# A three-product matmul order, the seams' sums, and the last loop step of a causal convolution

## The chip, the cores and the metric

One core of a Trainium2 chip runs the whole program. The metric is the device time of one execution in microseconds; the time before is the median of three executions. The engines that matter are PE (TensorE, the matmuls), DVE (VectorE), ACT (ScalarE) and SP, which issues the DMAs.

## The reference

Two layers, each a feed-forward part, a token mixer and another feed-forward part, on x of 512 tokens by 1024 channels in float32. Layer 0 mixes with a diagonal state-space model (S5), layer 1 with a causal depthwise convolution of 31 taps. Cut to what is computed:

```python
def swiglu(h, w1, w3, w2):
    return (silu(h @ w1) * (h @ w3)) @ w2

def s5_mixer(h, ...):
    u = h @ w_in
    ...
    z = y * sigmoid(y @ w_glu + b_glu)
    return z @ w_out

def conv_mixer(h, ...):
    a, g = split(h @ w_in + b_in, 2)
    z = a * sigmoid(g)
    z = causal_depthwise_conv(z, dw) + dw_b
    z = silu(layernorm(z, ln_g, ln_b))
    return z @ w_out + b_out

for i in range(2):
    h = swiglu(rmsnorm(x, norm_pre[i, 0]), ffn_w1[i, 0], ffn_w3[i, 0], ffn_w2[i, 0])
    x = x + 0.5 * rmsnorm(h, norm_post[i, 0])
    h = s5_mixer(rmsnorm(x, ...)) if i == 0 else conv_mixer(rmsnorm(x, ...))
    x = x + rmsnorm(h, norm_post[i, 1])
    h = swiglu(rmsnorm(x, norm_pre[i, 2]), ffn_w1[i, 1], ffn_w3[i, 1], ffn_w2[i, 1])
    x = x + 0.5 * rmsnorm(h, norm_post[i, 2])
```

## The kernel before

Channels lie on the 128 partitions, tokens in the free dimension; x is eight tiles of 128x512. Every large product is made from three fp32r matmuls (`mm3`, L115): the weight tile and the data are each split into a high part and a rest, and hi·xh, hi·xl and lo·xh are summed in one PSUM bank. L117, L118 and L119 are these three, in that order; L118 is the only one that reads xl, L119 the only one that reads lo. 

Weights come in units of 128x1024 float32 (512 KB), eight 128x128 tiles each, numbered through the program. `want(n)` (L97) splits all units up to n: ACT copies the high part (L101, CAST), DVE subtracts to get the rest (L105). The raw unit comes by a DMA that SP issues (L90). There are three raw buffers, so unit u+3 can be fetched only when the DVE subtraction of unit u has ended, and SP, which issues in program order, waits for it there. Each engine runs its instructions in the order in which the code emits them; that order, and nothing else, is what the change edits.

A sub-layer ends in `proj` (L262), whose last one or two outputs (`nl` of them) are made in two halves of 256 tokens, A and B, so that the norm of half A can start while half B is still being multiplied. Between two sub-layers lies a seam: a loop over `s`, two halves by eight k, in which `scaled` (L358) and `added` (L362) bring x up to date, `split_hi` (ACT, L180) and `split_lo` (DVE, L193) split it, and `entry_step` (L197) multiplies the piece with the first four weight units of the next sub-layer, twelve matmuls at a time. `stat` (L124) sums squares over the partitions with a matmul of ones; `rsqrt_steps` turns them into the factor y. With `defer`, the squares and sums of the new x are made behind the seam (128x512 each) instead of in it, and `entry_norm` (L245) makes y later, in the next sub-layer's loop. The six sub-layers are ffn, S5, ffn, ffn, conv, ffn, so there are five seams; seams 2 (after S5) and 5 (after conv) have nl=2, the others 1.

In S5, `glu_step` multiplies the gate's weights with one k of y for four outputs; `gates` then runs Sigmoid (ACT L1089), a product (DVE L1090), and a split of z (ACT L1093, DVE L1094). The output projection starts with a lead: for each k, four outputs of three matmuls, with the units of s_w_out that `want` splits behind the first gates.

In conv, the loop over i (2 to 7) multiplies 2 x 8 x 3 matmuls for output pair i on PE. On the other engines the pair before is gated (`gate`, DVE L1148 to L1164) and convolved. Channels 0, 1 and (26 taps of it) 7 are convolved on DVE, one tap an instruction (L1183, 128x512); the rest go over DRAM (`z_d`) into a layout in which PE convolves them with Toeplitz operators (`operators` fetches them, 2.25 MB for a channel tile; `banded` L1286 multiplies; `unstack` and `fetch` bring the result back over `c_d`). At i=7 the order is: operators(5), operators(6), `want(u0+19)`, which splits the first four units of the output projection (16 to 19), then `fetch`, gate(6), the taps that are due, and unstack of channel tile 4. After the loop come gate(7) and what is left of the taps and sums, and then a layer norm in two halves (L1403 to L1440), behind which the output projection starts.

Of the kernel before, what the change touches and what calls it, by code (L numbers as in the profile page):

```python
# [13 lines left out]
NK = 8  # L14
# [27 lines left out]
def trunk(ctx: ExitStack, tc: tile.TileContext, h, plan):  # L42
# [72 lines left out]
    def mm3(out, u, s, xh, xl, start, stop):  # L115
        hi, lo = halves[u]
        PE.matmul(out, lhsT=hi[:, s, :], rhs=xh, start=start, stop=False)  # L117
        PE.matmul(out, lhsT=hi[:, s, :], rhs=xl, start=False, stop=False)  # L118
        PE.matmul(out, lhsT=lo[:, s, :], rhs=xh, start=False, stop=stop)  # L119


    def stat(acc):
# [72 lines left out]
        )  # L195

    def entry_step(k, cs, xn, u0, ps4, outs=range(4)):  # L197
        for j in outs:
            mm3(ps4[j][:, cs], u0 + j, k, xn[k][:, 0, cs], xn[k][:, 1, cs], k == 0, k == NK - 1)

    def start(pre):

# [47 lines left out]

        rsqrt(stat(e["acc2"][:, HALVES[1]]), e["y"][:, HALVES[1]])

    def proj(u0, nk, rhs, post, nl, pre, xn, bias=None, lead=None, carried=None, defer=True, early=False):

        acc = stat_tile() if carried is None else carried
        acc2 = stat_tile()
# [2 lines left out]
        un = u0 + nk  # L259
# [28 lines left out]
        if lead is not None:  # L288
            want(unit(3, nk - 1)[0])
            ps4 = [psum() for _ in range(4)]  # L290
            for s in range(2 * nk + 2):
                ck = lead(s)
                if ck:
                    for m in range(4):
                        product(m, ck[1], ps4[m][:, ck[0]], ck[0])
            want(unit(4, nk - 1)[0])
            for m in range(4):
                evac(m, ps4[m], FULL)
                copy(m, ps4[m], FULL)
# [24 lines left out]
        for m in last:  # L324
# [2 lines left out]
                product(m, k, ps, A)  # L327
            evac(m, ps, A)
            copy(m, ps, A)
        psb = {}  # L330
        for i, (m, k) in enumerate((m, k) for m in last for k in range(nk)):
            if i == 5:
                sa = stat(acc[:, A])
                steps = rsqrt_steps(sa, y[:, A], carried is None)
                if pre is not None:
                    lo_engine[0] = None
                    want(un + 3)
                    lo_engine[0] = DVE
                for f in steps:
                    f()  # L340
            if k == 0:
                psb[m] = psum()[:, :n]
            product(m, k, psb[m], B)
            if k == nk - 1 and m != NK - 1:
                evac(m, psb[m], B)
                copy(m, psb[m], B)
        pb = psb[NK - 1]
        if pre is None:
            assert bias is None and carried is not None
# [21 lines left out]
        for s in range(len(todo) + 2):  # L371
            if s < len(todo):
                if s == NK:
                    while side:
                        side.pop(0)()
                scaled(*todo[s])
            if side:
                side.pop(0)()
            elif more and s > NK + 5:
                more.pop(0)()  # L380
            if 1 <= s <= len(todo):
                added(*todo[s - 1])
            if s == 4:
                sq = square(NK - 1, pb, B)
                plus(sq, B)
                sb = stat(acc[:, B])
            if s == 5:
                copy(NK - 1, pb, B)
            if s >= 2:
                cs, k = todo[s - 2]  # L390
                split_lo(k, cs, xn, pre)
                if s == 2:
                    want_late()
                if not defer:
                    x_plus(sqs.pop((cs.start, k)), cs, acc2)
                entry_step(k, cs, xn, un, ps4)
                if early and s == NK + 2:
                    ye = y_tile()
                    more = rsqrt_steps(stat(acc2[:, A]), ye[:, A])
            if s == 5:  # L400
                side = rsqrt_steps(sb, y[:, B], carried is None)
        if defer:
            want(un + 4)
            for k in range(NK):
                x_plus(x_square(k, FULL, acc2), FULL, acc2)
        return {"xn": xn, "ps": ps4, "acc2": acc2, "u": un, "y": ye}
# [477 lines left out]
    def s5(e, post, pre):  # L884
# [125 lines left out]

        def glu_step(j0, bank, k):
            if k >= 0:
                for j in range(4):
                    glu_part(j0, bank, j, k)

        def glu_part(j0, bank, j, k):
            mm3(bank[j], g0 + j0 + j, k, yhl[k][:, 0, :], yhl[k][:, 1, :], k == 0, k == NK - 1)
# [110 lines left out]
    def conv(e, post, pre):  # L1128
# [197 lines left out]
        for i in range(2, NK):  # L1326
            want(u0 + 2 * i + 1)
            pa, pb = psum(), psum()
            for j, ps in enumerate((pa, pb)):
                for k in range(NK):  # L1330
                    mm3(ps, u0 + 2 * i + j, k, xn[k][:, 0, :], xn[k][:, 1, :], k == 0, k == NK - 1)
                    if i == 2 and j == 0 and k == 4:
                        entry_norm(e)
                if j == 0 and i - 3 in banks:
                    done = banded(i - 3)
            if i - 2 in banks and i > 4:
                operators(i - 2)
            if i == NK - 1:
                operators(i - 1)
            want(u0 + 2 * i + (3 if i < NK - 1 else 5))  # L1340
            if i == 2:
                ACT.preload_act_table(AF.Sigmoid)
                for n in range(2):
                    gate(n, e["ps"][2 * n], e["ps"][2 * n + 1])
            else:
                fetch()
                gate(*pend)
            pend = i, pa, pb
            finish()
            if i == NK - 1:  # L1350
                dg = flat(page(F32))
                nc.sync.dma_start(out=dg[:, : (CONV_W - C_TAPS[i]) * P], in_=h["diag"])
            step(BUD_D[i - 2])
            accumulate()
            if done:
                unstack(*done)
                done = None
        done = [banded(i) for i in banks[-2:]]
        fetch()
        gate(*pend)  # L1360
# [45 lines left out]
        first = newton(0)  # L1406
        for n, c in enumerate(HALVES):
            ACT.activation(q[:, c], ps12[n][:, :256], AF.Square, scale=1.0 / 32)
            if n:
                first.pop(0)()  # L1410
            DVE.tensor_tensor(v[:, c], ps12[n][:, 256:], q[:, c], op=S)
            ACT.activation(y0[:, c], v[:, c], AF.Abs_reciprocal_sqrt, bias=eps)
            if n == 0:
                less(0, 0)
        ACT.preload_act_table(AF.Silu)
        for f in first:
            f()
# [61 lines left out]
    for i, (kind, idx) in enumerate(subs):  # L1479
        pre = subs[i + 1][1] * 8 if i + 1 < len(subs) else None  # L1480
        post = 48 + idx * 8
        if kind == "ffn":
            after = subs[i + 1][0] if i + 1 < len(subs) else "ffn"
            e = ffn(e, post, pre, after == "ffn", after == "s5")
        elif kind == "s5":
            e = s5(e, post, pre)
        else:
            e = conv(e, post, pre)
# [101 lines left out]
```

## Time and profile before

| | us |
|---|---|
| median of three executions | 1881.44 (1881.33 to 1881.71) |
| the profiled execution | 1881.37 |
| its span, first to last instruction | 1879.6 |
| DVE busy in the span | 1079.2 |
| ACT busy in the span | 639.1 |

The profiled execution's time is 1.8 us more than its span; that part lies around the instructions. Starts in the timeline are counted from the span's start. PE's ends are modelled and overlap: a row of PE tells by its start, not by its length, and the distance of two starts is the rate. A row of another engine with xN is N instructions that followed each other. The view by windows gives, for a stretch of time, the busy time and number of instructions of each engine, then the granted TensorE clock, the DMA share and GB/s.

### The profile page before, as it was taken

How to read it: one execution, taken by the hardware profiler on the slowest of the kernel's cores; microseconds unless marked ns; L12 is line 12 of the kernel's file. 1: busy time of each engine (PE TensorE's matmuls, PEld its weight loads, DVE VectorE, ACT ScalarE, POOL GpSimd, SP SyncE). 2: the span in 40 equal slices, each digit the busy share in tenths (PEclk: the TensorE clock that was granted, in tenths of full speed). 3: DMA queues.
4: the chain of work that ended last, by engine and by line, in shares of the span. 5: the costliest groups of instructions: out<-in, count | busy, mean ns of one | idle time of the engine just before them, and what ended most of it. 6: DMA issues, size and time to landing. Idle time of an engine off the chain costs nothing.

```text
span 1879.6 us, 24042 instructions
## 1 busy us (share of the span) xinstructions
PE 1861.2 (99%) x9498; PEld 1588.4 (85%) x9498; DVE 1079.2 (57%) x1907; ACT 639.1 (34%) x931; POOL 30.5 (2%) x56
## 2 busy tenths in 40 slices
PE   9999999999999999999999999999999999999998
PEld 7888888888989888888898888888887988888887
DVE  6888556789658543332485433325988775433324
ACT  5232545242245432221344222213413543222211
POOL 0000000003100000000000000000000000000000
PEclk9999999999999999999999999999999999999999
DMA  5344448849422423222223332222473224332321
GB/s 164 113 138 155 146 124 256 279 148 353 152 90 79 135 90 110 92 78 90 102 78 124 102 100 82 95 92 79 163 282 107 79 74 129 97 105 79 95 96 46
DMA packets 101809, 234.87 MB, mean 125 GB/s; under 512 B 26176, under 2 KB 45120, under 8 KB 101696
## 3 DMA queue, kind: packets, MB, share of 16 engines
q1 hardware_dynamic: 101552, 233.31, 38.0%
q8 instruction: 74, 1.21, 0.3%
q14 instruction: 39, 0.32, 0.1%
q10 hardware_dynamic: 144, 0.02, 0.0%
HBM read 209.58 MB, written 23.72 MB: 124 GB/s over the span
## 4 chain that ended last, share of the span: by engine, by line
PE 83%; DVE 12%; ACT 2%; issue 2%; DMA 1%; SPq 0%; DVEq 0%; ACTq 0%
PE ps L118 26%; PE ps L119 26%; PE ps L117 26%; DVE pg L105 1%; DVE pg L697 1%; PE ps L1286 1%; PE ps L976 1%; DVE pg L1183 1%; PE ps L792 1%; DVE pg L527 1%; DVE tmp L467 1%; PE ps L124 1%; ACT tmp L466 1%; DVE pg L699 1%; ACT pg L469 1%
## 5 line engine op out<-in xcount | busy, mean ns | idle before, releaser
L117 PE MATMUL ps<-pg,pg 128*128 128x512 f32 (+1 forms) x2808 | 1035.6, 369 | 4.5 <-ACT pg L1429 3.9
L118 PE MATMUL ps<-pg,pg 128*128 128x512 f32 (+1 forms) x2808 | 1030.8, 367 | 4.5 <-DVE pg L193 3.7
L119 PE MATMUL ps<-pg,pg 128*128 128x512 f32 (+1 forms) x2808 | 1028.5, 366 | 0.2 <-DVE pg L105 0.2
L118 PEld LDWEIGHTS ps<-pg,pg 128*128 128x128 f32 x2808 | 530.7, 189 | 94.7 <-DVE pg L193 7.5
L117 PEld LDWEIGHTS ps<-pg,pg 128*128 128x128 f32 x2808 | 530.8, 189 | 91.5 <-ACT pg L1429 4.3
L119 PEld LDWEIGHTS ps<-pg,pg 128*128 128x128 f32 x2808 | 530.6, 189 | 85.8 <-DVE pg L105 0.9
L105 DVE TENSOR_TENSOR pg<-raw,pg 128x1024 fp32r<-128x1024 f32 x305 | 361.2, 1222 | 106.2 <-ACT pg L101 68.0
L101 ACT CAST pg<-raw 128x1024 fp32r<-128x1024 f32 x310 | 311.4, 1047 | 107.3 <-PE ps L118 28.4
L467 DVE TENSOR_TENSOR tmp<-ps,tmp 128x512 f32<-128x512 f32 x88 | 60.9, 692 | 247.6 <-PE ps L119 218.4
L278 DVE TENSOR_TENSOR acc<-acc,tmp 128x512 f32<-128x512 f32 (+1 forms) x53 | 32.6, 615 | 250.1 <-ACT tmp L273 250.0
L466 ACT ACTIVATE tmp<-tmp 128x512 f32<-128x512 f32 x88 | 55.6, 632 | 287.0 <-DVE tmp L465 287.0
L469 ACT CAST pg<-tmp 128x512 fp32r<-128x512 f32 x88 | 54.6, 621 | 251.2 <-DVE tmp L467 249.4
L273 ACT ACTIVATE tmp<-ps 128x512 f32<-128x512 f32 (+1 forms) x45 | 24.2, 539 | 285.3 <-PE ps L119 284.9
L470 DVE TENSOR_TENSOR pg<-tmp,pg 128x512 fp32r<-128x512 f32 x88 | 61.0, 693 | 61.7 <-ACT pg L469 61.7
L465 DVE TENSOR_TENSOR tmp<-ps,y 128x512 f32<-128x512 f32 x88 | 60.6, 689 | 27.4 <-PE ps L119 27.4
L180 ACT ACTIVATE pg<-x,gsc 128x256 fp32r<-128x256 f32 x80 | 40.7, 509 | 68.1 <-DVE x L362 68.1
L1183 DVE SCALAR_TENSOR_TENSOR pg<-pg,vec,pg 128x512 f32<-128x512 f32 x82 | 55.4, 755 | 0.0
L193 DVE SCALAR_TENSOR_TENSOR pg<-x,gsc,pg 128x256 fp32r<-128x256 f32 (+1 forms) x88 | 44.8, 509 | 2.6 <-ACT pg L180 1.4
L1286 PEld LDWEIGHTS ps<-pg,pg 128*128 128x128 f32 x360 | 40.8, 192 | 0.3
L1286 PE MATMUL ps<-pg,pg 128*128 128x128 f32 x360 | 40.8, 275 | 0.0
L362 DVE SCALAR_TENSOR_TENSOR x<-tmp,gsc,x 128x256 f32<-128x256 f32 x80 | 38.8, 485 | 0.0
L976 PE MATMUL ps<-pg,pg 128*128 128x128 f32 x256 | 35.0, 277 | 1.2 <-DVE pg L962 0.9
(165 smaller groups left out, 828.6 us busy)
## 6 DMA issues: line engine op xcount, KB each, us to landing
raw<-w SPq DMA_DIRECT2D x262, 512.0 KB, 4.0
pg<-tab_d SPq DMA_DIRECT2D x24, 512.0 KB, 5.9
pg<-toep SPq DMA_DIRECT2D x20, 512.0 KB, 6.1
tab_d<-pg SPq DMA_DIRECT2D x16, 512.0 KB, 4.4
raw<-cv_w_in SPq DMA_DIRECT2D x16, 512.0 KB, 4.2
pg<-s5b SPq DMA_DIRECT2D x8, 512.0 KB, 6.5
pg<-f_d SPq DMA_DIRECT2D x32, 128.0 KB, 5.9
raw<-s_w_in SPq DMA_DIRECT2D x8, 512.0 KB, 3.8
```

Of the source, the lines that this page charges most:

```text
L101: ACT.copy(hv, r)
L105: lo_engine[0].tensor_tensor(lv, r, hv.bitcast(F32), op=ALU.subtract)
L117: PE.matmul(out, lhsT=hi[:, s, :], rhs=xh, start=start, stop=False)
L118: PE.matmul(out, lhsT=hi[:, s, :], rhs=xl, start=False, stop=False)
L119: PE.matmul(out, lhsT=lo[:, s, :], rhs=xh, start=False, stop=stop)
L465: DVE.tensor_tensor(a, pa, e["y"], op=ALU.mult)
L466: ACT.activation(a, a, AF.Silu)
L467: DVE.tensor_tensor(a, pb, a, op=ALU.mult)
L469: ACT.copy(t[:, 0, :], a)
L470: DVE.tensor_tensor(t[:, 1, :], a, t[:, 0, :].bitcast(F32), op=ALU.subtract)
L1183: DVE.scalar_tensor_tensor(a, v, dw(i, w), a, op0=M, op1=A)
L1286: PE.matmul(ps[:, q * P : q * P + P], lhsT=op[ND * q + d], rhs=z[:, q, 8 - d : 8 - d + P], start=d == 0, stop=d == ND - 1,)
```

## The change

`mm3` makes hi·xh, lo·xh, hi·xl instead of hi·xh, hi·xl, lo·xh. A new `mm3s` does the same for several outputs at once: first hi·xh and lo·xh of all of them, then hi·xl of all. `entry_step`, the lead of `proj` and S5's `glu_step` use it, with four outputs (the program's start with two and one).

At seams with nl=2, the statistic of half A is made two products earlier (i=3 for i=5); of output 6's half B only the square (ACT) stays where it was, and its sum and its copy (DVE) move into the seam's step s=2.

Into conv, `defer` is 5: the squares and sums of x move out of seam 4 behind the split of the sixth unit, and `entry_norm` moves from the fifth product of i=2's first output to the seventh of its second one, ten products later. The seams after the other feed-forward layers keep what they had (0 before S5, 4 between two).

In conv's step i=7, operators(6) and the four splits move to the end of the step, behind gate(6), the taps and unstack. In the layer norm behind the loop, both squares and variances are made before the two Abs_reciprocal_sqrt, and the first Newton step no longer stands between them.

```diff
@@ mm3 @@
         PE.matmul(out, lhsT=hi[:, s, :], rhs=xh, start=start, stop=False)
-        PE.matmul(out, lhsT=hi[:, s, :], rhs=xl, start=False, stop=False)
-        PE.matmul(out, lhsT=lo[:, s, :], rhs=xh, start=False, stop=stop)
+        PE.matmul(out, lhsT=lo[:, s, :], rhs=xh, start=False, stop=False)
+        PE.matmul(out, lhsT=hi[:, s, :], rhs=xl, start=False, stop=stop)
+
+    def mm3s(todo, xh, xl, start, stop):
+
+        for out, u, s in todo:
+            hi, lo = halves[u]
+            PE.matmul(out, lhsT=hi[:, s, :], rhs=xh, start=start, stop=False)
+            PE.matmul(out, lhsT=lo[:, s, :], rhs=xh, start=False, stop=False)
+        for out, u, s in todo:
+            PE.matmul(out, lhsT=halves[u][0][:, s, :], rhs=xl, start=False, stop=stop)
@@ entry_step @@
-        for j in outs:
-            mm3(ps4[j][:, cs], u0 + j, k, xn[k][:, 0, cs], xn[k][:, 1, cs], k == 0, k == NK - 1)
+        mm3s([(ps4[j][:, cs], u0 + j, k) for j in outs], xn[k][:, 0, cs], xn[k][:, 1, cs], k == 0, k == NK - 1)
@@ proj @@
-                    for m in range(4):
-                        product(m, ck[1], ps4[m][:, ck[0]], ck[0])
+                    c, k = ck
+                    outs = [(ps4[m][:, c], *unit(m, k)) for m in range(4)]
+                    mm3s(outs, rhs[k][:, 0, c], rhs[k][:, 1, c], k == 0, k == nk - 1)
...
-        psb = {}
+        psb, behind = {}, []
...
-            if i == 5:
+            if i == (5 if nl == 1 else 3):
...
             if k == nk - 1 and m != NK - 1:
-                evac(m, psb[m], B)
-                copy(m, psb[m], B)
+                behind.append((m, square(m, psb[m], B)))
...
+            if s == 2 and behind:
+                m, sq = behind.pop()
+                plus(sq, B)
+                copy(m, psb[m], B)
             if s == 4:
...
         if defer:
-            want(un + 4)
+            want(un + defer)
@@ s5 @@
         def glu_step(j0, bank, k):
             if k >= 0:
-                for j in range(4):
-                    glu_part(j0, bank, j, k)
+                mm3s([(bank[j], g0 + j0 + j, k) for j in range(4)], yhl[k][:, 0, :], yhl[k][:, 1, :], k == 0, k == NK - 1)
@@ conv @@
-                    if i == 2 and j == 0 and k == 4:
+                    if i == 2 and j == 1 and k == 6:
                         entry_norm(e)
...
-            if i == NK - 1:
-                operators(i - 1)
-            want(u0 + 2 * i + (3 if i < NK - 1 else 5))
+            if i < NK - 1:
+                want(u0 + 2 * i + 3)
...
                 unstack(*done)
                 done = None
+            if i == NK - 1:
+                operators(i - 1)
+                want(u0 + 2 * i + 5)
...
-            if n:
-                first.pop(0)()
             DVE.tensor_tensor(v[:, c], ps12[n][:, 256:], q[:, c], op=S)
-            ACT.activation(y0[:, c], v[:, c], AF.Abs_reciprocal_sqrt, bias=eps)
             if n == 0:
                 less(0, 0)
+        for c in HALVES:
+            ACT.activation(y0[:, c], v[:, c], AF.Abs_reciprocal_sqrt, bias=eps)
@@ main @@
-            e = ffn(e, post, pre, after == "ffn", after == "s5")
+            e = ffn(e, post, pre, {"ffn": 4, "conv": 5, "s5": 0}[after], after == "s5")
```

Three places show how instructions move. The lines of the changed kernel have other numbers: its matmuls L125 and L126 are hi·xh and lo·xh of `mm3s`, L128 its hi·xl; L133 is the statistic that was L124, L1159 and L1161 the gate's L1148 and L1150, L1257 the sum that was L1246.

First DVE, at conv's step i=7, from the four splits (L105, units 16 to 19) on. Before:

```order
L105 TENSOR_TENSOR pg_11177<-raw_10878,pg_11176 128x1024
L105 TENSOR_TENSOR pg_11183<-raw_11017,pg_11182 128x1024
L105 TENSOR_TENSOR pg_11189<-raw_11023,pg_11188 128x1024
L105 TENSOR_TENSOR pg_11195<-raw_11180,pg_11194 128x1024
L1148 TENSOR_TENSOR tmp_11206<-ps_10917,y_10541 128x512
L1150 TENSOR_TENSOR tmp_11205<-ps_10916,y_10541 128x512
L1153 SCALAR_TENSOR_TENSOR tmp_11205<-tmp_11205,vec,tmp_11206 128x512
L1156 MEMSET pg_11212 128x4x8
L1227 TENSOR_TENSOR pg_10482<-pg_10482,acc_10486 128x512
L1225 SCALAR_TENSOR_TENSOR pg_10483<-pg_10483,vec,acc_10486 128x512
L1245 TENSOR_TENSOR pg_10487<-pg_10482,pg_10483 128x512
L1246 TENSOR_TENSOR pg_10487<-pg_10487,tmp_11222 128x512
```

The next row there is gate(7)'s first, L1148. With the change, from gate(6)'s second row on:

```order
L1161 TENSOR_TENSOR tmp_11149<-ps_10894,y_10549 128x512
L1164 SCALAR_TENSOR_TENSOR tmp_11149<-tmp_11149,vec,tmp_11150 128x512
L1167 MEMSET pg_11156 128x4x8
L1238 TENSOR_TENSOR pg_10472<-pg_10472,acc_10476 128x512
L1236 SCALAR_TENSOR_TENSOR pg_10473<-pg_10473,vec,acc_10476 128x512
L1256 TENSOR_TENSOR pg_10477<-pg_10472,pg_10473 128x512
L1257 TENSOR_TENSOR pg_10477<-pg_10477,tmp_11166 128x512
L105 TENSOR_TENSOR pg_11185<-raw_10856,pg_11184 128x1024
L105 TENSOR_TENSOR pg_11191<-raw_10995,pg_11190 128x1024
L105 TENSOR_TENSOR pg_11197<-raw_11001,pg_11196 128x1024
L105 TENSOR_TENSOR pg_11203<-raw_11188,pg_11202 128x1024
L1159 TENSOR_TENSOR tmp_11288<-ps_11048,y_10549 128x512
```

The four splits stood ahead of gate(6) and now stand behind it and its sums, directly ahead of gate(7) (the last row).

Second PE, at the first step of S5's output lead: banks ps_4764 to ps_4767 are the four outputs, pg_4645 is z's first tile, and pg_4702/4703, pg_4708/4709, pg_4714/4715, pg_4720/4721 are the hi and lo of four weight units. Before:

```order
L117 MATMUL ps_4764<-pg_4645,pg_4702 128x512
L118 MATMUL ps_4764<-pg_4645,pg_4702 128x512
L119 MATMUL ps_4764<-pg_4645,pg_4703 128x512
L117 MATMUL ps_4765<-pg_4645,pg_4708 128x512
L118 MATMUL ps_4765<-pg_4645,pg_4708 128x512
L119 MATMUL ps_4765<-pg_4645,pg_4709 128x512
L117 MATMUL ps_4766<-pg_4645,pg_4714 128x512
L118 MATMUL ps_4766<-pg_4645,pg_4714 128x512
L119 MATMUL ps_4766<-pg_4645,pg_4715 128x512
L117 MATMUL ps_4767<-pg_4645,pg_4720 128x512
L118 MATMUL ps_4767<-pg_4645,pg_4720 128x512
L119 MATMUL ps_4767<-pg_4645,pg_4721 128x512
```

With the change:

```order
L125 MATMUL ps_4764<-pg_4645,pg_4702 128x512
L126 MATMUL ps_4764<-pg_4645,pg_4703 128x512
L125 MATMUL ps_4765<-pg_4645,pg_4708 128x512
L126 MATMUL ps_4765<-pg_4645,pg_4709 128x512
L125 MATMUL ps_4766<-pg_4645,pg_4714 128x512
L126 MATMUL ps_4766<-pg_4645,pg_4715 128x512
L125 MATMUL ps_4767<-pg_4645,pg_4720 128x512
L126 MATMUL ps_4767<-pg_4645,pg_4721 128x512
L128 MATMUL ps_4764<-pg_4645,pg_4702 128x512
L128 MATMUL ps_4765<-pg_4645,pg_4708 128x512
L128 MATMUL ps_4766<-pg_4645,pg_4714 128x512
L128 MATMUL ps_4767<-pg_4645,pg_4720 128x512
```

The fourth unit's lo (pg_4721) was read by the twelfth matmul of the step and is now read by the eighth; the four products with z's low part stand at the end.

Third PE, in conv's step i=2: the statistic from which y is made (acc_9362), between the products of the two outputs. Before, in the first output:

```order
L117 MATMUL ps_10522<-pg_8248,pg_10488 128x512
L118 MATMUL ps_10522<-pg_8248,pg_10488 128x512
L119 MATMUL ps_10522<-pg_8248,pg_10489 128x512
L124 MATMUL ps_10539<-acc_9362,ones 128x512
L117 MATMUL ps_10522<-pg_8317,pg_10488 128x512
L118 MATMUL ps_10522<-pg_8317,pg_10488 128x512
L119 MATMUL ps_10522<-pg_8317,pg_10489 128x512
```

With the change, in the second output:

```order
L117 MATMUL ps_10501<-pg_8386,pg_10444 128x512
L118 MATMUL ps_10501<-pg_8386,pg_10445 128x512
L119 MATMUL ps_10501<-pg_8386,pg_10444 128x512
L133 MATMUL ps_10547<-acc_9362,ones 128x512
L117 MATMUL ps_10501<-pg_8455,pg_10444 128x512
L118 MATMUL ps_10501<-pg_8455,pg_10445 128x512
L119 MATMUL ps_10501<-pg_8455,pg_10444 128x512
```

The statistic stands 30 matmuls of 128x512 later in PE's order.

More of the change, by code (lines that the diff above doesn't have):

```diff
@@ L251, in entry_rest, with proj @@
         rsqrt(stat(e["acc2"][:, HALVES[1]]), e["y"][:, HALVES[1]])
-    def proj(u0, nk, rhs, post, nl, pre, xn, bias=None, lead=None, carried=None, defer=True, early=False):
+    def proj(u0, nk, rhs, post, nl, pre, xn, bias=None, lead=None, carried=None, defer=4, early=False):
         acc = stat_tile() if carried is None else carried
@@ L457, in last_half, with ffn @@
             added(B, k)
-    def ffn(e, post, pre, defer=True, early=False):
+    def ffn(e, post, pre, defer=4, early=False):
         u0, xn = e["u"], e["xn"]
```

## The prediction

> **What bounds the kernel now.** I read the page's busy times and the chain that ended last, then PE's waits, then the stretches where PE is not dense.
>
> ```profile
> PE 1861.2 (99%) x9498; PEld 1588.4 (85%) x9498; DVE 1079.2 (57%) x1907; ACT 639.1 (34%) x931; POOL 30.5 (2%) x56
> PE 83%; DVE 12%; ACT 2%; issue 2%; DMA 1%; SPq 0%; DVEq 0%; ACTq 0%
> ...
> PE ps L117 <- ACT pg L1429: 3.9, 1, 3.9
> PE ps L118 <- DVE pg L193: 3.7, 11, 0.6
> ```
>
> PE is busy nearly all the time, but the second line says that 12% of the chain runs through DVE: there PE keeps busy without setting the end. The waits name few places: the layer norm's first row (L1429), and xl (L193) eleven times, at the seams. No matmul is removed, so the change can only gain what is lost at such places, or lose at places that are dense.
>
> **The rate.** Two starts tell it.
>
> ```profile
> 530.04 0.39 PE L117 MATMUL ps<-pg,pg 128*128 128x512 f32 x1
> 530.27 0.39 PE L118 MATMUL ps<-pg,pg 128*128 128x512 f32 x1
> ...
> 531.63 0.39 PE L118 MATMUL ps<-pg,pg 128*128 128x512 f32 x1
> ...
> 532.86 0.50 PE L119 MATMUL ps<-pg,pg 128*128 128x512 f32 x1 [0.16 <-DVE pg L105]
> 533.20 0.40 PE L117 MATMUL ps<-pg,pg 128*128 128x512 f32 x1
> ```
>
> A 128x512 matmul takes (531.63-530.04)/7 = 0.227 us, whether its weights repeat those before (L117 to L118) or not (L118 to L119); a new order by itself costs nothing. A 128x256 takes 0.12 (574.83 to 574.95 in the next fence).
>
> **Seams.** Windows give what each lost: the stretch less its matmuls at 0.12.
>
> ```profile
> 386.00:410.00 24.00, 23.03 (x174) 21.42 (x173) 21.71 (x59) 12.24 (x30) 0.11 (x1) 1.00 0.37 141
> 570.00:582.00 12.00, 10.53 (x79) 9.62 (x78) 9.53 (x24) 4.53 (x10) 0.00 (x0) 1.00 0.31 102
> 1300.00:1316.00 16.00, 15.37 (x118) 14.35 (x118) 14.78 (x39) 7.42 (x20) 0.00 (x0) 1.00 0.10 33
> 1500.00:1510.00 10.00, 8.32 (x61) 7.46 (x60) 9.03 (x23) 3.74 (x9) 0.00 (x0) 1.00 0.17 60
> ...
> 574.83 0.28 PE L118 MATMUL ps<-pg,pg 128*128 128x256 f32 x1
> 574.95 0.28 PE L119 MATMUL ps<-pg,pg 128*128 128x256 f32 x1
> ...
> 578.35 0.39 PE L118 MATMUL ps<-pg,pg 128*128 128x256 f32 x1 [0.57 <-DVE pg L193]
> ...
> 580.35 0.70 PE L124 MATMUL ps<-acc,ones 128*128 128x256 f32 x2 [0.42 <-DVE acc L278]
> ```
>
> Seam 1 lost 24.0-174x0.12 = 3.1, seam 2 2.5, seam 4 1.8, seam 5 2.7; some tenths of each are the float32 statistics.
> - Seam 1 (into S5): the first product with xl was second in its step and is ninth, 7x0.12 = 0.84 later. DVE keeps its work, and the lateness on it adds up along the seam, so I take **-0.8**; 0 to -2.4 (most of its loss) are the ends.
> - Seams 2 and 5: the statistic of A is two products earlier, and the sum and copy (two rows of some 0.33 us) are out of the way of the first `scaled`. But they come back at s=2 ahead of split_lo, and the first step now needs the fourth unit's lo at its eighth matmul. What is late next is the statistic of B (580.35), behind ACT's square. **-0.6** and **-0.55**, ends 0 and -1.5 each.
> - Seam 3: waits show nothing there; 0.
> - Seam 4: without squares PE leaves it up to 1.9 earlier; but conv behind it is bound by DVE (below), so 0 of its own.
> - The program's start: its pieces need lo0 a matmul earlier and xl later; **-0.1**.
>
> **S5's output lead.** The rows that lead to PE's wait at 532.86:
>
> ```profile
> 519.42 1.37 ACT L1089 ACTIVATE tmp<-ps,vec 128x512 f32<-128x512 f32 x2 [6.71 <-PE ps L119]
> 524.59 2.95 ACT L101 CAST pg<-raw 128x1024 fp32r<-128x1024 f32 x3
> 530.49 1.05 ACT L101 CAST pg<-raw 128x1024 fp32r<-128x1024 f32 x1 [2.96 <-DMA raw<-s_w_out]
> ...
> 526.98 6.18 SPq L90 DMA_DIRECT2D raw<-s_w_out  x4
> ...
> 525.72 3.50 DVE L105 TENSOR_TENSOR pg<-raw,pg 128x1024 fp32r<-128x1024 f32 x3 [0.32 <-ACT pg L101]
> 531.58 1.23 DVE L105 TENSOR_TENSOR pg<-raw,pg 128x1024 fp32r<-128x1024 f32 x1 [2.36 <-ACT pg L101]
> ```
>
> Sigmoid (519.42) starts when the gate's first output is done. In the order before, that output's last product is the third matmul of the last `glu_step`; now it is the ninth: 6x0.227 = 1.36 later. ACT then runs without a gap up to the casts of three units; the first unit's subtraction (525.72 to 526.94) frees a raw buffer, SP fetches the fourth (526.98, 3.5 us), it is cast (530.49) and its rest is ready at 532.81. All of it moves by 1.36, to 534.17. PE needs that rest at the lead's eighth matmul, 530.04+7x0.227 = 531.63, where it had been the twelfth. It waits 2.5 us; the eighth and four more matmuls bring the next step to 534.17+5x0.227+0.1 = 535.4, for 533.20 before. **+2.3**. If Sigmoid's shift were hidden, it would be 532.86+1.23-533.20 = +0.9: these are the ends.
>
> **Conv.** DVE's windows and the rows around gate(7):
>
> ```profile
> 1336.00:1402.00 66.00, 66.00 (x364) 57.10 (x363) 64.61 (x98) 15.85 (x19) 0.00 (x0) 1.00 0.70 241
> 1421.00:1447.00 26.00, 26.00 (x179) 22.86 (x178) 25.72 (x40) 6.33 (x9) 0.00 (x0) 1.00 0.38 103
> ...
> 1332.37 1.02 PE L124 MATMUL ps<-acc,ones 128*128 128x512 f32 x2
> ...
> 1336.40 0.69 DVE L1148 TENSOR_TENSOR tmp<-ps,y 128x512 f32<-128x512 f32 x1
> 1401.56 2.36 DVE L105 TENSOR_TENSOR pg<-raw,pg 128x1024 fp32r<-128x1024 f32 x2
> 1406.75 1.22 DVE L105 TENSOR_TENSOR pg<-raw,pg 128x1024 fp32r<-128x1024 f32 x1 [2.83 <-issue]
> 1413.76 1.22 DVE L105 TENSOR_TENSOR pg<-raw,pg 128x1024 fp32r<-128x1024 f32 x1 [5.78 <-ACT pg L101]
> 1420.41 0.69 DVE L1148 TENSOR_TENSOR tmp<-ps,y 128x512 f32<-128x512 f32 x1 [0.62 <-PE ps L119]
> ...
> 1402.81 12.53 SPq L90 DMA_DIRECT2D raw<-cv_w_out  x4
> 1412.68 1.05 ACT L101 CAST pg<-raw 128x1024 fp32r<-128x1024 f32 x1 [10.28 <-DMA raw<-cv_w_out]
> ...
> 1414.68 0.48 PE L117 MATMUL ps<-pg,pg 128*128 128x512 f32 x1
> ...
> raw<-w SPq DMA_DIRECT2D x262, 512.0 KB, 4.0
> ...
> GB/s 86 139 154 136 398 417 421 407 428 389 438 421 417 431 407 389 417 421 435 403 318 37 9 14 89 337 340 119 0 105 293 201 19 61 28 125 159 228 266 107
> ```
>
> DVE is full from gate(0) (1336.40) to 1402 and from gate(7) (1420.41) to 1447; between them it idles 2.83+5.78+0.62 = 9.2 us, inside and behind the splits. The statistic (1332.37) moves 30x0.227 = 6.8 later in PE's order, less the 1.9 that seam 4 gives: gate(0) comes 4.9 later, and all DVE work up to 1402 with it, to about 1406.5. That alone would fit into the 9.2 of idle time. The squares and sums that leave seam 4 run in the 6.8 us by which the statistic is later. gate(6) and its sums then run 1406.5 to about 1411.5.
>
> The splits now come behind them. ACT must first unstack channel tile 4, whose bank is full when PE turns to L117 (1414.68, at best 1412.8 now). So unit 16 is cast from 1413.4 and its rest ends about 1415.7. Only then can unit 19 be fetched, and SP has operators(6) ahead of it, which waits for the reads of gate(6)'s z behind it: about 1417.3, where the row of before has 1402.81. There unit 19 took until 1412.6, behind 2 x 2.25 MB of operators at some 0.42 MB/us; now 2.25 MB are ahead and units 20 and 21 beside it, 3.75 MB, 9 us from 1415: it lands about 1423.8. Cast and subtraction, 2.3 us by the rows 1412.68 to 1414.98, end at 1426.1. gate(7) stands right behind that subtraction on DVE and everything else of conv behind gate(7), 26 us without a gap: **+5.7**. On SP, behind unit 19, stand the fetches of 20 to 22, the last waiting for 19's rest, and then tile 4's store to c_d, whose reader on DVE moves with gate(7); so no more is added there. PE runs the last operators and diagonals under that stretch, and its own lateness is covered. Had it landed after 4.0 us, the page's median for such a fetch, gate(7) would stand at 1417.3+4.0+2.3 = 1423.6, +3.2; with operators(6) and its reads costing SP nothing, at 1421.4, +1.0; with nothing in its favour at 1427.3, +6.9.
>
> **Layer norm behind conv.**
>
> ```profile
> 1453.76 0.58 PE L117 MATMUL ps<-pg,pg 128*128 128x256 f32 x1 [3.86 <-ACT pg L1429]
> 1454.85 0.58 PE L118 MATMUL ps<-pg,pg 128*128 128x256 f32 x1 [0.51 <-DVE pg L1440]
> ...
> 1448.60:1452.00 3.40, 1.30 (x6) 0.80 (x5) 2.23 (x6) 2.01 (x6) 0.00 (x0) 1.00 0.00 0
> 1452.00:1455.40 3.40, 1.13 (x3) 0.84 (x4) 3.26 (x11) 3.32 (x6) 0.00 (x0) 0.50 0.00 0
> ```
>
> The wait for xl at 1454.85, 0.9 beyond the rate, goes, and the first row comes about 0.5 earlier when the two root rows stand together: **-1.4**, ends -0.5 and -1.7.
>
> **Sum**: -0.1-0.8-0.6+2.3+5.7-1.4-0.55 = +4.5 on the profiled execution's 1881.37 (which stands 0.07 below the median): 1885.9.
>
> **The clock.** The two windows show the granted clock at 0.50 after a stretch of 3.4 us with 1.30 of PE work. The new idle time in S5's lead, 2.5 of 3.4, would leave 0.9. If it drops there, 3.4 us run at half rate: +1.7. A single place is thin ground, so it is not in the sum. [...]
>
> **Rivals.**
> - Late split (forecast): 1883.5 to 1888. For it: one raw buffer chain, read from rows. Chance 0.47.
> - The clock drops at S5's lead as well: 1885.9+1.7 = 1887.6, at most 1889.5. Chance 0.15.
> - Unit 19 is hidden: SP reaches its fetch early, it lands before DVE has done the other splits, and gate(7) waits for PE as at 1420.41. Conv +0 to +1, and the sum without 5.7 is -1.2: 1880.2 to 1881.2, not slower. It decides if the fetch lands before 1418.7. For it: 9.2 us of idle time; against it: lo of 16 not before 1415.7. Chance 0.26.
> - Neither S5's shift nor unit 19 shows: only the seams and the layer norm count, 1881.4-3.5 = 1877.9. Chance 0.12.
>
> A measurement of this kernel can tell about 0.2%, 3.8 us, from no change: 1877.7 and 1885.2 are the bounds. Of the forecast about two thirds (0.32) lie above 1885.2, with the clock's 0.15 that is 0.47 slower; half of the last case, and a little for seams that gain up to their ends, is 0.08 faster; the rest 0.45 within. The range takes 1879 (unit 19 hidden, seams somewhat better) to 1889.5.
>
> **What would show it.** In the changed profile: a DVE idle time before the last L105 ahead of gate(7), ended by a raw fetch, and gate(7) after 1423; Sigmoid at about 520 in S5 and a PE wait of over 2 us for L105 near 531; L193 gone from most of PE's waits; no wait for L1440. If gate(7) starts by 1421, the forecast is wrong by about its 5.7; if S5's lead shows no wait over 1 us, by 1.4 more.

## The result, and the profile after

The changed kernel takes **1893.13 us** (median of four executions, 1889.61 to 1894.66), the one before 1881.56 beside it: the ratio is 1.0059, with a 95% interval of 1.0047 to 1.0072. That is 11.6 us slower, where 4.5 had been forecast, and outside the range given (1879 to 1889.5). The profiled execution took 1893.44, its span is 1891.7.

The page of the changed kernel, busy times and the chain that ended last:

```profile
PE 1863.8 (99%) x9498; PEld 1588.7 (84%) x9498; DVE 1078.9 (57%) x1900; ACT 638.0 (34%) x923; POOL 30.6 (2%) x56
...
PE 83%; DVE 11%; DMA 2%; ACT 2%; issue 2%; SPq 1%; DVEq 0%; ACTq 0%
```

No engine has noticeably more work. The chain has new shares for DMA (2% for 1%) and for SP's queue (1% for 0%): the loss is waiting for transfers. Comparing the start of each matmul by its number in PE's order with the kernel before shows where time comes from. From before the first seam to the end of seam 1 it gains 1.7 us; it loses 2.7 at S5's output lead and 1.3 at half clock behind it, gains 0.6 at seam 2 and 1.9 at seam 4, loses 12.3 from there to the first product behind conv's layer norm, 1.0 more in the output projection, and gains 0.7 at seam 5.

PE's waits of the changed kernel (what waited, for what, then total, times and longest):

```profile
PE ps L1264 <- DVE pg L1236: 8.1, 3, 6.6
PE ps L125 <- ACT pg L1441: 3.4, 1, 3.4
PE ps L133 <- DVE acc L286: 1.8, 2, 0.9
PE ps L1264 <- DVE pg L1402: 1.7, 1, 1.7
PE ps L125 <- ACT pg L101: 1.4, 1, 1.4
PE ps L126 <- DVE pg L113: 1.2, 2, 0.6
```

L193, eleven times in the list of before, is gone under its new number (L202) but for 0.2. New is that PE waits for DVE's sums at the end of conv (L1264 for L1236): DVE is late there. DVE's timeline in conv (start, duration, line; in brackets the idle time before it and what ended it):

```profile
1342.70 0.69 DVE L1159 TENSOR_TENSOR tmp<-ps,y 128x512 f32<-128x512 f32 x1
...
1407.92 0.69 DVE L1159 TENSOR_TENSOR tmp<-ps,y 128x512 f32<-128x512 f32 x1
...
1409.39 0.75 DVE L1164 SCALAR_TENSOR_TENSOR tmp<-tmp,vec,tmp 128x512 f32<-128x512 f32 x1 [0.19 <-ACT tmp L1160]
...
1416.02 3.50 DVE L105 TENSOR_TENSOR pg<-raw,pg 128x1024 fp32r<-128x1024 f32 x3 [3.21 <-ACT pg L101]
1431.67 1.22 DVE L105 TENSOR_TENSOR pg<-raw,pg 128x1024 fp32r<-128x1024 f32 x1 [12.16 <-ACT pg L101]
1432.82 0.68 DVE L1159 TENSOR_TENSOR tmp<-ps,y 128x512 f32<-128x512 f32 x1
```

gate(0) is at 1342.70, 34.6 behind seam 4's second statistic (1308.08), where it was 29.4 before (1336.40-1307.01): 5.2 later, for 4.9 forecast. gate(6) is at 1407.92, 1.4 behind the forecast. Three splits follow, then DVE stands for 12.16 us in front of the fourth, and gate(7) comes at 1432.82 where it had come at 1420.41. That is the wait of the forecast, at twice its size: 12.4 for 5.7. SP's queue and ACT show why:

```profile
1402.58 2.55 SPq L1288 DMA_DIRECT2D pg<-toep  x5
1405.23 1.90 SPq L1316 DMA_DIRECT2D c_d<-pg  x4
1412.84 0.34 SPq L1317 DMA_DIRECT2D pg<-c_d  x1
1413.28 0.38 SPq L1165 DMA_DIRECT2D z_d<-tmp  x1
1416.46 1.74 SPq L1170 DMA_DIRECT2D pg<-z_d  x4
1418.25 0.43 SPq L1362 DMA_DIRECT2D pg<-diag  x1
1419.02 2.46 SPq L1288 DMA_DIRECT2D pg<-toep  x5
1421.57 11.68 SPq L90 DMA_DIRECT2D raw<-cv_w_out  x4
...
1430.60 1.04 ACT L101 CAST pg<-raw 128x1024 fp32r<-128x1024 f32 x1 [12.71 <-DMA raw<-cv_w_out]
```

Read it from the bottom. Unit 19 (the first of the four L90) is asked for at 1421.57 and cast at 1430.60, 9.0 us later. Ahead of it on SP stand operators(6) (toep) and the reads of gate(6)'s z, and these could not start before 1416.46, because z's store was issued at 1413.28 only. Its data were ready at 1410.14 (L1164, 1409.39+0.75), 3.1 us earlier: the read of c_d at 1412.84 stood ahead of it on SP, and that one waited until its own four stores (issued from 1405.23 to 1407.13, behind 2.25 MB of operators) had landed.

At S5's lead, the matmuls that waited, and Sigmoid, which now follows L128, the last of the new order:

```profile
530.93 0.50 PE L125 MATMUL ps<-pg,pg 128*128 128x512 f32 x1 [1.45 <-ACT pg L101]
532.19 0.50 PE L126 MATMUL ps<-pg,pg 128*128 128x512 f32 x1 [0.76 <-DVE pg L105]
532.52 1.47 PE L128 MATMUL ps<-pg,pg 128*128 128x512 f32 x4
533.78 0.63 PE L125 MATMUL ps<-pg,pg 128*128 128x512 f32 x1
534.21 0.63 PE L126 MATMUL ps<-pg,pg 128*128 128x512 f32 x1
...
518.70 1.27 ACT L1100 ACTIVATE tmp<-ps,vec 128x512 f32<-128x512 f32 x2 [8.19 <-PE ps L128]
```

PE waits 1.45+0.76 us for the fourth unit, and then two starts lie 0.43 apart, not 0.227: the clock. Windows of the seams and of these stretches (us, then PE, PEld, DVE, ACT and POOL busy, granted clock, DMA share, GB/s):

```profile
386.00:410.00 24.00, 23.68 (x185) 22.62 (x184) 22.65 (x59) 12.08 (x31) 0.10 (x1) 1.00 0.35 134
570.00:582.00 12.00, 10.61 (x84) 10.09 (x83) 9.91 (x24) 4.91 (x11) 0.00 (x0) 1.00 0.48 168
1300.00:1316.00 16.00, 16.00 (x134) 15.95 (x134) 15.05 (x39) 5.85 (x13) 0.00 (x0) 1.00 0.10 34
...
529.60:533.00 3.40, 1.32 (x5) 0.86 (x6) 2.09 (x3) 2.44 (x4) 0.00 (x0) 1.00 0.87 284
533.10:536.40 3.30, 3.30 (x10) 2.53 (x9) 3.22 (x6) 2.93 (x6) 0.00 (x0) 0.50 0.52 160
...
1464.90:1468.30 3.40, 2.71 (x12) 2.71 (x13) 3.37 (x11) 3.04 (x7) 0.00 (x0) 0.50 0.00 0
1468.30:1471.70 3.40, 3.40 (x18) 3.40 (x17) 3.40 (x12) 3.00 (x8) 0.00 (x0) 0.50 0.00 0
```

Seam 1 holds 185 matmuls in the 24 us where it held 174; seam 4 is dense (134x0.12 = 16.1). At half clock (0.50), S5's lead runs for one window of 3.41 us, and the layer norm's first products for two, 6.83 us, as before, only that PE now works in nearly all of both. Two more windows, 1444.4 to 1451.2, are at half clock too, behind the 6.6 us in which PE waits for DVE's sums; the kernel before has none there. PE waits for DVE again at 1451.48 (0.86 us), so this drop does not set the end.

### The profile page after: what moved, and what is told of

It reads as the page before. It is cut to its first block, busy times and chain, and to the rows that moved or that the text cites. A ratio compares the mean times of both kernels' runs of the same rounds, so it can differ in the third digit from the quotient of the medians.

```text
span 1891.7 us, 24032 instructions
## 1 busy us (share of the span) xinstructions
PE 1863.8 (99%) x9498; PEld 1588.7 (84%) x9498; DVE 1078.9 (57%) x1900; ACT 638.0 (34%) x923; POOL 30.6 (2%) x56
## 4 chain that ended last, share of the span: by engine, by line
PE 83%; DVE 11%; DMA 2%; ACT 2%; issue 2%; SPq 1%; DVEq 0%; ACTq 0%
PE ps L118 23%; PE ps L117 23%; PE ps L119 23%; PE ps L126 3%; PE ps L128 3%; PE ps L125 3%; DVE pg L105 2%; DVE pg L709 1%; PE ps L988 1%; PE ps L1297 1%; DVE pg L1194 1%; PE ps L804 1%; DVE pg L539 1%; DVE tmp L479 1%; PE ps L133 1%
## 5 line engine op out<-in xcount | busy, mean ns | idle before, releaser
L117 PE MATMUL ps<-pg,pg 128*128 128x512 f32 (+1 forms) x2328 | 885.4, 380 | 0.0
L118 PE MATMUL ps<-pg,pg 128*128 128x512 f32 (+1 forms) x2328 | 880.7, 378 | 0.6 <-DVE pg L105 0.4
L119 PE MATMUL ps<-pg,pg 128*128 128x512 f32 (+1 forms) x2328 | 880.4, 378 | 0.0
L118 PEld LDWEIGHTS ps<-pg,pg 128*128 128x128 f32 x2328 | 438.0, 188 | 84.0 <-DVE pg L105 1.9
L117 PEld LDWEIGHTS ps<-pg,pg 128*128 128x128 f32 x2328 | 438.0, 188 | 82.5 <-issue 1.4
L119 PEld LDWEIGHTS ps<-pg,pg 128*128 128x128 f32 x2328 | 437.9, 188 | 81.6
L105 DVE TENSOR_TENSOR pg<-raw,pg 128x1024 fp32r<-128x1024 f32 x305 | 360.9, 1220 | 109.1 <-ACT pg L101 73.8
L286 DVE TENSOR_TENSOR acc<-acc,tmp 128x512 f32<-128x512 f32 (+1 forms) x53 | 32.5, 614 | 248.3 <-ACT tmp L281 248.2
L125 PE MATMUL ps<-pg,pg 128*128 128x256 f32 (+1 forms) x480 | 138.1, 313 | 5.2 <-ACT pg L1441 3.4
L126 PE MATMUL ps<-pg,pg 128*128 128x256 f32 (+1 forms) x480 | 136.7, 310 | 2.4 <-DVE pg L113 1.2
L125 PEld LDWEIGHTS ps<-pg,pg 128*128 128x128 f32 x480 | 93.6, 195 | 10.0 <-ACT pg L1441 3.8
L126 PEld LDWEIGHTS ps<-pg,pg 128*128 128x128 f32 x480 | 93.5, 195 | 8.5 <-DVE pg L226 1.6
L128 PE MATMUL ps<-pg,pg 128*128 128x256 f32 (+1 forms) x480 | 91.6, 308 | 0.2 <-DVE pg L202 0.2
L128 PEld LDWEIGHTS ps<-pg,pg 128*128 128x128 f32 x480 | 71.8, 193 | 4.4 <-DVE pg L202 0.6
```

What stands on the lines that cost most here:

```text
L105: lo_engine[0].tensor_tensor(lv, r, hv.bitcast(F32), op=ALU.subtract)
L118: PE.matmul(out, lhsT=lo[:, s, :], rhs=xh, start=False, stop=False)
L119: PE.matmul(out, lhsT=hi[:, s, :], rhs=xl, start=False, stop=stop)
L126: PE.matmul(out, lhsT=lo[:, s, :], rhs=xh, start=False, stop=False)
L128: PE.matmul(out, lhsT=halves[u][0][:, s, :], rhs=xl, start=False, stop=stop)
```

## The experiments

The theory to begin with was the forecast's: DVE's queue stands behind the late fetch of unit 19 (theory 1). Its rival was that the later norm into conv makes the whole chain behind it late (theory 2, called so from the second set on). Times are medians; the ratio is to the kernel before beside it.

**The conv move undone, in part and whole, and alone.**

```diff
 a_conv_back: the changed kernel with
+            if i == NK - 1:
+                operators(i - 1)
-            if i < NK - 1:
-                want(u0 + 2 * i + 3)
+            want(u0 + 2 * i + (3 if i < NK - 1 else 5))
...
-            if i == NK - 1:
-                operators(i - 1)
-                want(u0 + 2 * i + 5)
 b_want_back: only want back, operators at the end
 c_oper_back: only operators back, want at the end
 d_conv_alone: the kernel before with only this move
```

> The changed kernel with operators(6) and the four splits back ahead of gate(6) at conv's last loop step; all else as changed. Theory 1 (the fetch of unit 19 is late, and DVE's queue stands behind it): gate(7) falls from 1432.7 us to 1420 to 1422, and the time by 9 to 12 us, to 1881 to 1884. Rival (DVE is late because the norm into conv is made 4.9 us later, and the place of the splits matters little): gate(7) stays above 1428, the time above 1889.

> Only the four splits back ahead of gate(6); operators(6) stays at the end of the step. Theory 1 says the splits' place decides and not operators(6): the time is that of a_conv_back within 1.5 us, 1881 to 1885. Rival (operators(6), fetched late, holds up PE's last Toeplitz product and so the end): still above 1888.

> Only operators(6) back ahead of gate(6); the four splits stay at the end of the step. If the wait for unit 19 is made of two parts, the queue of SP and 2.25 MB ahead of it, and the splits' late start, this takes the first part away: unit 19 is asked for at about 1417 instead of 1421.4 and lands 4 to 5 us later instead of 9: gate(7) at 1424 to 1425, time 1884.5 to 1886.5. If the late splits alone decide, 1890 to 1893 remains.

> The kernel before with nothing but the move of operators(6) and the four splits to the end of the step. Theory 1: unit 16 still cannot be cast before channel tile 4 is unstacked (about 1415), so unit 19 comes late here too: gate(7) at 1428 to 1432, time 1888 to 1892. Rival (only together with the later norm does it hurt): 1881 to 1884.

| | us | ratio, 95% |
|---|---|---|
| a_conv_back | 1890.48 | 1.0049 (1.0036 to 1.0061) |
| b_want_back | 1887.11 | 1.0034 (1.0022 to 1.0047) |
| c_oper_back | 1892.29 | 1.0056 (1.0044 to 1.0069) |
| d_conv_alone | 1886.68 | 1.0026 (1.0014 to 1.0037) |

a, b and d missed what theory 1 expected; b and d lie between its range and the rival's, a in the rival's, and c came where late splits alone had put it. The move alone costs about 5 us (d), and yet to undo it gives only 2.7 back (a). So something else in the change costs more, and the two don't add. In a_conv_back, SP and DVE:

```profile
1403.18 8.01 SPq L1288 DMA_DIRECT2D pg<-toep  x10
1412.11 11.47 SPq L90 DMA_DIRECT2D raw<-cv_w_out  x4
...
1421.99 1.23 DVE L105 TENSOR_TENSOR pg<-raw,pg 128x1024 fp32r<-128x1024 f32 x1 [11.43 <-ACT pg L101]
1423.14 0.69 DVE L1159 TENSOR_TENSOR tmp<-ps,y 128x512 f32<-128x512 f32 x1
```

With the splits in their old place unit 19 is late again, asked for at 1412.11 where it was at 1402.81 before: SP's operators start 7 us later (1403.18 for 1396.14), since they stand behind the reads of z, and z is late with the gates. Now even gate(6) (1423.14) is behind it, and PE waits 9.3 us for its z. c_oper_back shows that operators(6) ahead of unit 19 are not the price either: fetched early, they sit ahead of the c_d stores and of z, and unit 19 is asked for later still (1425.76).

In b_want_back gate(7) comes as early as in the kernel before, and yet the time is 6 us above it:

```profile
1420.32 0.69 DVE L1159 TENSOR_TENSOR tmp<-ps,y 128x512 f32<-128x512 f32 x1
...
PE ps L1297 <- DMA pg<-toep: 5.6, 1, 5.6
```

Here PE waits for operators(6) in the Toeplitz product (L1297). That is the rival that its expectation names, though the time lies 0.9 below that rival's bound. So an early gate(7) is not enough: operators and z must come early as well.

**The norm into conv and S5's gate put back.**

```diff
 g_norm_old: the changed kernel with
-                    if i == 2 and j == 1 and k == 6:
+                    if i == 2 and j == 0 and k == 4:
                         entry_norm(e)
-            e = ffn(e, post, pre, {"ffn": 4, "conv": 5, "s5": 0}[after], after == "s5")
+            e = ffn(e, post, pre, {"ffn": 4, "conv": 0, "s5": 0}[after], after == "s5")
 e_glu_old: the changed kernel with
-                mm3s([(bank[j], g0 + j0 + j, k) for j in range(4)], ...)
+                for j in range(4):
+                    glu_part(j0, bank, j, k)
 i_best_norm: g_norm_old, e_glu_old and a_conv_back together
 k_best_all: i_best_norm, and S5's lead in the old order (product) too
```

> The changed kernel with the norm into conv as before (squares and sums in seam 4, the statistic after the fifth product of the first output of i=2); the splits stay last in the loop step. Theory 2 (the later norm shifts the whole chain gate, z over DRAM, operators, fetch of unit 19 by 5 to 7 us and is the main cost; the moved splits alone cost the 5 us of d_conv_alone): conv costs about 5 instead of 10 us, the time falls from 1893 to 1887 to 1889. Theory 1 alone (late splits set the loss): stays above 1891.

> The changed kernel with only S5's glu_step in the old order of products. The step of the forecast (Sigmoid starts 1.36 us later, and the chain to the lead's fourth unit with it): PE's wait in the lead shrinks by 1.2 to 1.5 us, and the half clock behind it goes in the runs that had it: time lower by 1.3 to 2.8 us than the changed kernel. Rival (the lead's own order makes all of the wait): lower by less than 0.4.

> The changed kernel with the norm into conv as before, the splits and operators(6) ahead of gate(6) as before, and S5's glu_step in the old order of products; what stays of the change are the new order of products in the seams, the leads and all other matmuls, the moved sums at seams 2 and 5, and the layer norm's order. Theory 2: conv loses nothing and its layer norm gains about 1; seams gain 2.0+0.6+0.6, S5's lead loses about 1: 1876.5 to 1879. Rival (the splits' cost comes from elsewhere in conv, from the new product order): above 1881.

> As i_best_norm, and S5's output lead in the old order of products too. If the lead's eight early products are what makes PE wait for the fourth unit's rest, this gives back what is lost there, 0.9 to 1.2 us: 1875.5 to 1878, and PE's wait in the lead is the 0.16 us of before.

| | us | ratio, 95% |
|---|---|---|
| g_norm_old | 1886.20 | 1.0023 (1.0014 to 1.0032) |
| e_glu_old | 1890.79 | 1.0046 (1.0033 to 1.0058) |
| i_best_norm | 1878.13 | 0.9980 (0.9971 to 0.9989) |
| k_best_all | 1877.65 | 0.9981 (0.9973 to 0.9990) |

e_glu_old and i_best_norm came as expected, g_norm_old 0.8 us below its bounds. k_best_all lies in its bounds, but gave back 0.5 where 0.9 to 1.2 were expected, and PE's wait in the lead is 0.37, not 0.16. With both parts of conv and the order in glu_step undone, the rest of the change is 3.6 us faster than the kernel before, with the lead's order undone too, 4.1. The old order in glu_step takes 2.3 us off the changed kernel's median: PE's wait in the lead falls from 2.21 to 0.8, and with it the half clock (the mean granted clock of the profiled execution is 0.996, for 0.995). With the lead's old order, 0.4 is left of that wait, and the median is 0.5 lower.

**What of the later norm costs, and whether unit 19 is all of the moved splits' price.**

```diff
 q_own19: the changed kernel with
+            r = flat(page(F32)) if ptr["dma"] in own else rawp.tile([P, 1024], F32, tag="raw", name=nm("raw"))
...
             if i < NK - 1:
                 want(u0 + 2 * i + 3)
+            else:
+                own.append(u0 + 19)
+                w_dma(u0 + 19)
 m_norm_late: k_best_all with only entry_norm at j == 1, k == 6
 n_defer_only: k_best_all with only "conv": 5
 o_mm3_old: k_best_all with mm3 (not mm3s) in the old order
```

> The changed kernel, but weight unit 19 gets a buffer of its own and SP issues its fetch at the start of the end of conv's last step, where before the change want stood; the splits themselves stay last. This takes the late fetch away and nothing else. Theory 1 (DVE stands behind unit 19 only): gate(7) at about 1420.5 instead of 1432.7, time 1881 to 1883.5. Theory 2 (the whole chain of z, operators and c_d is late, and unit 19 was only what came last): gate(7) early, but DVE then waits for c_d and PE for the last operators, as with the splits alone put back (1887.1): 1884.5 to 1888.

> k_best_all (1877.65) with only the statistic of the norm into conv ten products later; squares and sums stay in seam 4. Theory 2: the later place of the statistic is what shifts the chain: 1884 to 1888. If it is the moved squares and sums on DVE instead: below 1879.

> k_best_all with only the squares and sums moved out of seam 4 (behind the sixth unit's split); the statistic stays after the fifth product. Seam 4 gains its 1.3 to 1.9 us, but PE now meets the statistic before DVE has the sums: PE waits there 2 to 5 us, and gate(0) comes 2 to 4 us later than in k_best_all: 1880 to 1886. If gate(0) is not later by over 1 us: 1876 to 1878.

> k_best_all with mm3's old order of the three products wherever four outputs are not taken together; the seams keep the new order. In the output projection behind conv all kernels with the new order lost 0.7 to 1.0 us against before, with a wait of the second product for a unit's rest (L105) that the old order needs one matmul, 0.23 us, later. Theory: this comes back, 1876.6 to 1877.2. Rival (a late fetch behind conv, not the order): 1877.4 to 1878.

| | us | ratio, 95% |
|---|---|---|
| q_own19 | 1885.49 | 1.0016 (1.0007 to 1.0025) |
| m_norm_late | 1888.12 | 1.0032 (1.0020 to 1.0043) |
| n_defer_only | 1875.98 | 0.9972 (0.9961 to 0.9982) |
| o_mm3_old | 1877.61 | 0.9980 (0.9970 to 0.9990) |

The later statistic alone costs 10.5 us (1888.12 for 1877.65); the squares and sums moved out of seam 4 cost nothing and gain 1.7: the expected wait at the statistic did not come, and n_defer_only is the fastest so far. In m_norm_late, SP, DVE and two waits:

```profile
1406.28 11.86 SPq L90 DMA_DIRECT2D raw<-cv_w_out  x4
1418.20 1.93 SPq L1321 DMA_DIRECT2D c_d<-pg  x4
1424.24 0.34 SPq L1322 DMA_DIRECT2D pg<-c_d  x1
1424.68 0.37 SPq L1170 DMA_DIRECT2D z_d<-tmp  x1
...
1416.56 1.23 DVE L105 TENSOR_TENSOR pg<-raw,pg 128x1024 fp32r<-128x1024 f32 x1 [8.04 <-ACT pg L101]
1417.70 0.68 DVE L1164 TENSOR_TENSOR tmp<-ps,y 128x512 f32<-128x512 f32 x1
...
PE ps L1302 <- DMA pg<-z_d: 6.3, 1, 6.3
...
DVE pg L1241 <- DMA pg<-c_d: 4.6, 2, 3.8
```

Here the splits are in their old place and unit 19 lands late; gate(6) (1417.70) stands behind it, its z goes to DRAM at 1424.68 only, PE waits 6.3 us for it in the last Toeplitz product, and DVE 4.6 us for the results from c_d. That is a second price of a late conv chain: gate(7) itself is only 4.9 later than in k_best_all (1422.51 for 1417.58), the rest of the 10.5 stands behind these waits. It also fits that the two costs don't add: with the splits last, gate(6) and its z are earlier (1407.92 and 1413.28 in the changed kernel), and PE's wait for z is not in its list.

q_own19 says how much of the changed kernel's loss is unit 19: with an early fetch gate(7) comes at 1418.48, and the median falls by 7.6, into the range of theory 2; DVE then waits 3.4 us for c_d. The profiled execution is the fastest of eleven (1881.92, in the range of theory 1), so its trace does not show what the other 3.6 us of the median are. Where its expectation speaks of the start of the end of the step, the place meant is the one in the diff. o_mm3_old's median missed what its theory expected and lies in its rival's range; in the trace the wait behind conv fell from 0.4 (n_defer_only) to 0.2, too little to be seen.

**The moved splits with an early norm.** s_late_splits is n_defer_only with operators(6) and the splits last, as in the change; r_late_own19 adds q_own19's edit.

> n_defer_only (1875.98) with operators(6) and the four splits last in conv's step, as in the change. As in d_conv_alone the splits cost some 5 us if nothing else is late: 1880 to 1882, gate(7) 6 to 9 us later than the 1416.5 of n_defer_only. If their cost hung on the late norm: below 1878.

> s_late_splits, but unit 19 has a buffer of its own and is fetched early. If the moved splits cost nothing but unit 19's late fetch: gate(7) at or ahead of 1417 and the time of n_defer_only within 1.5 us, 1874.5 to 1877.5. If the place of the splits or operators(6) costs by itself: 1879 or more.

| | us | ratio, 95% |
|---|---|---|
| s_late_splits | 1881.13 | 0.9996 (0.9987 to 1.0005) |
| r_late_own19 | 1876.41 | 0.9972 (0.9961 to 0.9983) |

DVE in s_late_splits:

```profile
1421.18 1.23 DVE L105 TENSOR_TENSOR pg<-raw,pg 128x1024 fp32r<-128x1024 f32 x1 [5.06 <-ACT pg L101]
1422.32 0.68 DVE L1164 TENSOR_TENSOR tmp<-ps,y 128x512 f32<-128x512 f32 x1
```

And in r_late_own19, where the fourth split reads the unit's own buffer:

```profile
1412.47 3.50 DVE L107 TENSOR_TENSOR pg<-raw,pg 128x1024 fp32r<-128x1024 f32 x3 [10.02 <-DMA pg<-toep]
1415.88 1.22 DVE L107 TENSOR_TENSOR pg<-pg,pg 128x1024 fp32r<-128x1024 f32 x1
1417.02 0.68 DVE L1166 TENSOR_TENSOR tmp<-ps,y 128x512 f32<-128x512 f32 x1
```

Both came as expected. The move costs 5.1 us, and 4.7 of them go when unit 19 is fetched early: with an early norm nearly all of the move's cost is that one fetch. The fourth split follows the third without a gap, and gate(7) is at 1417.02 for 1422.32. In s_late_splits z and the operators are out of SP's way by 1411.64, and unit 19 is asked for at 1413.88, when the first split has ended. The hold behind the read of c_d, which makes the request late in the changed kernel, decides only together with the late norm.

## Why the prediction was right or wrong

- **Direction of conv, and the wait that costs: right.** DVE waits in front of the last L105 for unit 19, gate(7) behind it, all of conv behind gate(7). q_own19, s_late_splits and r_late_own19 show it.
- **Size of conv: wrong, and this is the step that failed**: "operators(6) ahead of it, which waits for the reads of gate(6)'s z behind it: about 1417.3", and a landing at about 1423.8. Measured: 1421.57, and a cast at 1430.60; the term of +5.7 became 12.4. The request was 4.3 late, mainly because a step was left out: on SP, z's store stands behind the read of c_d, which waits for stores that lie behind the operators of the step before. That held the store 3.1 us. Another 1.4 were there at gate(6) already (1407.92 for 1406.5), 1.1 of them came in with PE, late from S5; the two make 4.5, 0.2 too much. The landing took 9.0 us for the 6.5 forecast: from 1419.00 to 1430.60 the DMAs moved 345 GB/s, where the forecast had taken some 420 (0.42 MB/us). 4.3+2.5 is the missing 6.7 of gate(7), to 0.1. The hold on SP is read from the trace; no run moves that read alone. With the norm put back (g_norm_old) unit 19 is asked for at 1416.59 and gate(7) comes at 1424.22, 0.7 and 1.9 ahead of the forecast: what it missed belongs to the later norm, which it took for hidden.
- **"That alone would fit into the 9.2 of idle time": wrong.** m_norm_late loses 10.5 by the late statistic alone, 4.9 of it at gate(7). The idle time stood in front of splits whose fetches are issued behind the gates' own DMAs; when the gates came later, so did the fetches, and the idle time moved along instead of shrinking. The prediction treated it as slack.
- **S5's output lead: right in chain and nearly in size.** Sigmoid starts at 518.70; as PE is 2.1 ahead there, that is the 1.36 of the forecast. The step to the next product lost 2.7, for 2.3; the cast's wait of 1.45 and the rest's 0.76 are the two ends of the chain described. The half clock was left out of the sum as a rival; it came in the profiled execution, at 1.3 for the 1.7 forecast. e_glu_old undoes 2.3 of both.
- **Seam 1: right in sign, too small.** It gained 1.7, for 0.8, within the ends given. Nearly all of PE's waits for xl went, where the forecast had counted one shift of 0.84 for the whole seam.
- **Seams 2 and 5: right**, 0.6 and 0.7 for 0.6 and 0.55. What came late next was the statistic of B, as said (L133 for L286 in the list of waits).
- **Seam 4: right**, 1.9, and worth nothing in the changed kernel; but as n_defer_only shows, worth 1.7 when conv's statistic stays early.
- **The layer norm behind conv: right in kind.** The wait for xl behind the first row is gone; in k_best_all the stretch from the end of conv's sums into the layer norm's products gained 1.8 (from 2.7 to 4.4 ahead of the kernel before), for 1.4, but its half clock there lasts one window, not two (the mean granted clock of the profiled execution is 0.999, for 0.998 before). In the changed kernel, with two, the same stretch gained 0.5 (from 12.3 to 11.8 behind).
- **The output projection behind conv** was forecast at nothing and lost 0.7 to 1.0 in every kernel with the new order. A wait for a unit's rest of 0.4 is part of it, and the old order halves that; the remainder wasn't traced further.
- **Left open**: why executions of the changed kernel differ by 5 us (1889.61 to 1894.66). At S5's lead a drop of the clock is worth 1.3; the rest is not traced, since only one execution is profiled. In q_own19, which spreads by 6 us, the four executions with a mean granted clock of 0.999 took 1881.9 to 1885.1 and the five with 0.997 took 1885.5 to 1887.8, so the clock goes with part of such a spread there.

## What to carry to other kernels

Idle time of an engine is slack only if what ends it does not move when the engine's earlier work moves: follow the releaser back over the DMA queue to who issues it, and behind what. On SP, which issued in order, a single waiting read held every later fetch (in the changed kernel nothing was issued from 1407.13 to 1412.84, where the read of c_d waited), so list everything between the moved step and the place it moves to, with its waits, before a landing is priced. When two parts of a change each cost time at one place, measure each alone and both: here 5 and 10.5 us made 12.7 (e_glu_old less i_best_norm), and to undo one of them looked almost useless.

## What the runs showed of the hardware

In the changed kernel the granted clock fell to half at S5's lead behind a stretch in which most of the wait lay: from 529.60 to 533.00 PE had 1.32 us of work in 3.40, and the next 3.4 us ran at 0.50. In a_conv_back the same two waits, of 1.43 and 0.76, lay across two stretches:

```profile
527.60:530.90 3.30, 2.62 (x12) 1.85 (x10) 1.63 (x2) 0.34 (x1) 0.00 (x0) 1.00 0.79 247
531.00:534.30 3.30, 1.89 (x7) 1.33 (x8) 2.58 (x4) 2.57 (x5) 0.00 (x0) 1.00 0.73 241
```

No drop followed: the clock was 1.00 from 530.00 to 536.00. With the same lead, c_oper_back ran at 0.50 behind 3.40 us with 1.71 us of PE work (528.30 to 531.70), while b_want_back, with 1.94 in 3.30 (527.80 to 531.10), stayed at 1.00.

The record of the clock of the changed kernel has three stretches at half clock before the last matmul: they start at 533.05, 1444.40 and 1464.88 and last 3.41, 6.83 and 6.83 us, and the starts lie 267 and 6 times 3.413 us apart. The kernel before has one, of 6.83 us, from 1452.00. Laid out in steps of 3.413 us from these starts, up to the last matmul, the two traces show what stood in the step at full clock ahead of each drop: 1.32 us of PE work in the kernel before, and 1.37, 0.00 and 0.74 in the changed one. Of the other steps at full clock one had 1.67 (1458.06 to 1461.47, changed kernel) and all the rest 2.28 or more, and none of them was followed by half clock. There was no drop behind 1.67 here and one behind 1.71 in c_oper_back: PE's time is modelled, and the amount of work alone does not part the two cases. What else decides was not shown.
